# Operands in PSUM for one MLP and a modulation, other places for early products and for lower parts: a two-layer diffusion backbone

## The chip, the core and the metric

The kernel runs on one core of a Trainium2 chip. The core has five engines that work side by side, each through its own list of instructions in order: TensorE (PE in the profile, with its weight loads as PEld), VectorE (DVE), ScalarE (ACT), GpSimd (POOL) and SyncE (SP), which here only issues DMAs. They pass work on by semaphores, and they share two on-chip memories: SBUF, and PSUM, into whose banks of 128 x 512 floats the matmuls write. The metric is the device time of one execution in microseconds (us).

## The reference

A batch of one with 1024 latent tokens and 256 context tokens, width 1024, goes through two layers. Each layer derives six vectors for the latents and six for the context from a condition vector (`mod_l`, `mod_c`), normalises and modulates, mixes tokens (layer 0: a convolution module; layer 1: grouped attention), adds the gated result, and then runs an MLP with squared ReLU, again modulated and gated. After the last layer the context is dropped. Cut to what the change touches:

```python
sc = jax.nn.silu(c)
scc = jax.nn.silu(c_ctx)
for i in range(DEPTH):                                   # DEPTH = 2
    mod_l = jnp.split(sc @ w_mod[i] + b_mod[i], 6, axis=-1)
    mod_c = jnp.split(scc @ w_mod[i] + b_mod[i], 6, axis=-1)
    ...                                                  # norm, conv (0) or attention (1)
    ...
def sq_relu_mlp(h, w1, w2):                              # width 1024 -> 4096 -> 1024
    return jnp.square(jax.nn.relu(h @ w1)) @ w2
```

## The kernel before

**Three products for one.** Activations lie with channels on the 128 partitions and tokens along the free axis. Every large matmul is done in a float format that keeps only part of a float32, so each operand is held in two parts: the high part (a copy by ACT into that format) and the lower part (value minus high part). A product is then three matmuls: high x high, lower x high, high x lower (`mm3`, `prod`). For weights, `unit` (line 189) loads a 128 x 1024 tile `raw` by a DMA on SP, ACT writes the high part (line 205), and POOL the lower part (line 208) into `wsp` or, for each sixth unit, into `wx`. For activations the lower part is made on DVE or POOL.

**Layer 0** goes over three blocks b of up to 432 tokens. The convolution of a block (`conv_block`) is 31 taps on DVE (line 550), accumulated in PSUM banks named `cv`. The MLP (`mlp`, line 417 on) goes in eight chunks c of four hidden tiles f: for each f the product lands in a PSUM bank `ps`; ACT does the Relu into `r` and two Squares: one rounded into the high part `ht` (tile `hb` in the profile), one in full into `s`; DVE writes the lower part s - ht into `hb` (line 433). Then PE multiplies `hb` with `w2`, and DVE adds the gated sums to the stream `X` (line 455). PE takes its operands in program order, so a late `hb` or a late `X` (which frees a bank) holds PE up.

**The modulation of layer 1** is no matmul. `mods` (line 336) spreads the condition over all partitions (`sc`, 128 x 1024, Silu at line 341) and, for each 128 x 512 piece of the weights (`rawh`, loaded at line 347, three buffers), has DVE multiply it with half of `sc` and sum along the free axis (line 356, which the profile lists as a custom operation, with a short one that reads out the sum). 128 of them run as background work beside the MLP of block b = 1: a generator, `modq`, yields the estimated DVE time of each step and `pump` resumes it at fixed places of the foreground code. So the order on each engine is fixed when the program is built. Small additions and multiplications of 128 x 8 (lines 360, 331, 334) end each of the eight vectors.

**The MLP of layer 1** (`mlp1`, line 1186) forms its products by a scheme with seven half-size products instead of eight, on operands named B11, B21, T1, T3, T2, B22 and T4. While the second normalisation (`norm1`, line 1252 on, background work) prepares T1 to T4, PE runs "early" products for the first eight hidden tiles j: a first half with B11 into bank `b1`, copied to `p1` by ACT (line 1308), and a second half with B21 that goes on in the same bank. The second half of j-1 comes behind the first half of j. In the main loop `w1_ops` issues loads and splits with a priority that places them `AH1` = 190 places earlier than the code stands.

**The last product** (`ff2`, line 1407) goes over four chunks and, in each, over the seven operands. For each operand two activation tiles `tf` (list `tu`) and two weight tiles `raw` (list `wu`) are split: ACT writes the high part (line 1421) and DVE or POOL the lower part (line 1422, 128 x 1024). PE multiplies (line 1180), and DVE adds banks to sums (lines 1427, 1429). Which engine makes a lower part is set by two expressions at lines 1463 and 1475; G is POOL, V is DVE.

Of the kernel before, what the change touches and what calls it, by code (L numbers as in the profile page):

```python
# [117 lines left out]
NP = NF // 2  # L118
CP2 = 4
NPRO = 8  # L120
AH1, AH2 = 190, 200
PB = 2.5
OPS = ("B11", "B21", "T1", "T3", "T2", "B22", "T4")

# [1 line left out]
class Kern:  # L126
# [209 lines left out]
    def mods(self, i1, chunks, cond, dst):  # L336

        nc = self.nc
        sc = self.t("sc", [P, D], "sc")
        nc.sync.dma_start(out=sc, in_=self.A[cond].broadcast_to([P, D]))  # L340
        nc.scalar.activation(sc, sc, AF.Silu)
        units = [(j, u, z) for j in chunks for u in range(8) for z in range(2)]

        def load(i):
            j, u, z = units[i]
            raw = self.t(("ks", "vt", "sb")[i % 3], [P, 512], "rawh")
            nc.sync.dma_start(out=raw, in_=self.A["wmod1"][j * 8 + u, :, z * 512:z * 512 + 512])
            return raw
        raws = [load(0), load(1)]
        for i, (j, u, z) in enumerate(units):  # L350
            if i + 2 < len(units):
                raws.append(load(i + 2))
            if u == z == 0:
                part = self.t("mp", [P, 2, 8], "mp")
            raw = raws.pop(0)
            nc.vector.tensor_tensor_reduce(raw, raw, sc[:, z * 512:z * 512 + 512], 1.0, 0.0, ALU.mult, ALU.add,  # L356
                                           accum_out=part[:, z, u:u + 1])
            yield MQ
            if u == 7 and z:
                nc.vector.tensor_tensor(part[:, 0], part[:, 0], part[:, 1], ALU.add)  # L360
                self.mod_done(i1, j, dst, part[:, 0])
                self.mdone.add((i1, cond, j))
                yield 0.2
# [53 lines left out]
    def mlp(self, i, X, h, N, segs, gates, budget, hook=None, done=None, eng=None, off=False, each=None,  # L417
# [3 lines left out]
        for c in range(NF // CH):  # L421
            hT = []
            for f in range(c * CH, c * CH + CH):
                w = self.unit(self.A["w1"][i, f], eng)
                ps = self.psm()
                self.mm3(ps[:, :N], self.kpairs(w, h, N))
                r = self.t("tmp", [P, 512], "r")
                s = self.t("tmp", [P, 512], "s")
                ht = self.hts[f % 4]
                nc.scalar.activation(r[:, :N], ps[:, :N], AF.Relu)  # L430
                nc.scalar.activation(ht[:, 0, :N], r[:, :N], AF.Square)
                nc.scalar.activation(s[:, :N], r[:, :N], AF.Square)  # L432
                nc.vector.tensor_tensor(ht[:, 1, :N], s[:, :N], ht[:, 0, :N].bitcast(F32), ALU.subtract)  # L433
                hT.append(ht)
                self.pump(budget)
                if each:
                    each()
# [87 lines left out]
    def conv_block(self, b):  # L525
# [8 lines left out]
        for c2 in range(0, KT, 2):  # L534
# [17 lines left out]
            for z in range(2):  # L552
                v = u[:, c2 + z, off + 30:off + 30 + N]
                if c2 + z == 0:
                    nc.scalar.activation(vs[:, :N], v, AF.Copy)
                else:
                    nc.gpsimd.tensor_tensor(vs[:, :N], vs[:, :N], v, ALU.add)
        yield G3[2]
        mu = self.ps("rb", "mu")
        nc.tensor.matmul(mu[:, :N], lhsT=self.onesd, rhs=vs[:, :N], start=True, stop=True)  # L560
# [55 lines left out]
    def layer0(self):  # L616
# [3 lines left out]
        self.h1, self.u, self.udone, self.s1, self.X, self.h2 = {}, {}, {}, {}, {}, {}  # L620

        self.mdone = set()
        self.cc = self.t("cc", [P, KT, 2], "cc")
        nc.sync.dma_start(out=self.cc, in_=self.A["ccol"])
        nc.scalar.activation(self.cc, self.cc, AF.Silu)
# [560 lines left out]
    def mlp1(self, at, pre, r0):  # L1186
# [108 lines left out]
            nc.sync.dma_start(out=self.hd[OPS.index(o), :, j], in_=s)  # L1295

        halves = lambda w: [(lambda k: w[0](k), lambda k: w[1](k)), (lambda k: w[0](4 + k), lambda k: w[1](4 + k))]
        late = None

        def second(j, b1, a12):  # L1300
            self.prod(b1, a12, piece("B21"), False)
            hidden(b1, self.t("tmp", [P, 512], "s11"), j, "B11")
        for j in range(NPRO):
            a11, a12 = halves(self.unit(self.A["w1"][1, 2 * j]))
            b1 = self.ps("mm", "b1")
            p1 = self.t("tmp", [P, 512], "p1")
            self.prod(b1, a11, piece("B11"), True)
            nc.scalar.activation(p1, b1, AF.Copy)
            nc.sync.dma_start(out=self.p1d[:, j], in_=p1)
            if j:  # L1310
                self.pump(PB)
                second(*late)
            late = j, b1, a12
            if j:
                self.pump(PB)
        second(*late)
        while self.bg:
            self.pump(8.0)

# [1 line left out]
        ring = [work[:, 4 + i] for i in range(4)]  # L1321

        def w1_ops(j):
            with self.tc.high_priority(AH1):
                ra, rb = [self.t("raw", [P, 1024], "raw") for _ in range(2)]
                nc.sync.dma_start(out=ra, in_=self.A["w1"][1, 2 * j])
                nc.sync.dma_start(out=rb, in_=self.A["w1"][1, 2 * j + 1])
# [79 lines left out]
    def ff2(self, X):  # L1407
# [40 lines left out]
        for c in range(NC):  # L1448
# [6 lines left out]
            for what, y, first in ending if last else order:  # L1455
                with self.tc.high_priority(AH2):
                    tu, wu = [], []
                    z = {"B11": 0, "B21": 1, "T4": 3}.get(what)
                    for i in range(2):
                        f = self.t("raw", [P, 1024], "tf")  # L1460
                        nc.sync.dma_start(out=f.rearrange("p (i n) -> p i n", i=2),
                                          in_=self.hd[OPS.index(what), :, c * CP2 + 2 * i:c * CP2 + 2 * i + 2])
                        tu.append(unit(f, V if c == 0 and what == "B11" and i else G))
                    for i in range(2):
                        h = slice(1024 * i, 1024 * i + 1024)
                        s = S[:, h]
# [5 lines left out]
                            V.tensor_tensor(s, raw[1][:, h], s, ALU.subtract)  # L1472
                        elif what == "T3":
                            V.tensor_tensor(s, raw[0][:, h], raw[2][:, h], ALU.subtract)  # L1474
                        wu.append(unit(s if z is None else raw[z][:, h], G if z in (1, 3) or i and (z == 0 or last and what == "T1") else V))
                    xs = []
                    if c == NC - 2 and what in blocks:
                        _, blk, r = blocks[what]
# [143 lines left out]
```

## Time and profile before

| what | us |
|---|---|
| time, median of 3 runs (lowest, highest) | 2970.96 (2965.88, 2971.44) |
| the profiled execution: its time | 2970.38 |
| its span, first to last instruction | 2968.6 |
| PE busy in the span | 2779.6 |
| DVE busy | 2156.9 |
| POOL busy | 1709.4 |
| ACT busy | 1486.3 |

The profile is of one execution. The page gives each engine's busy time, the span in 40 slices, the chain of work that ended last, and the costliest groups of instructions, each with the idle time of its engine just before it and what released it. Beside the page the trace answers narrower questions: the waits of one engine by what ended them, the busy times of a window, the durations of one line's instructions, and the timeline. An idle engine costs nothing unless PE, the busiest one, waits for it later. A few rows in which matmuls, the main work, are seen to fill most of each slice but the first (each digit is the busy share of a fortieth of the span, in tenths; PEclk is the granted clock of TensorE, also in tenths):

```profile
PE   7999999999888899998998899999999889999999
PEclk9999999999998999999999999999999999999999
```

The first four slices in a row where PE's digit is 8 are 742 to 1039 us: the stretch in which the modulation of layer 1 runs beside the MLP of block 1.

### The profile page before, as it was taken

The numbers are of one execution on the slowest core, as the hardware profiler recorded it, in microseconds if no ns is written. First come the engines' busy times: TensorE is split into PE (matmuls) and PEld (weight loads), VectorE is DVE, ScalarE is ACT, GpSimd is POOL, SyncE is SP. The second block draws the span as 40 slices with busy tenths as digits, with TensorE's granted clock in tenths as the row PEclk, the third lists the DMA queues.
The fourth block names the chain that finished last, engine by engine and source line by source line (L and its number), as shares of the span: only waits on it lengthen the run. The fifth ranks groups of instructions, "written<-read, shape, count | busy, mean of one in ns | idle before, by whom it ended". The sixth has DMA issues, their size and how long they took to land. (4 is left out here: it accounts for less than half of the span.)

```text
span 2968.6 us, 36063 instructions
## 1 busy us (share of the span) xinstructions
PE 2779.6 (94%) x12634; PEld 2338.2 (79%) x12634; DVE 2156.9 (73%) x3224; ACT 1486.3 (50%) x2383; POOL 1709.4 (58%) x959
## 2 busy tenths in 40 slices
PE   7999999999888899998998899999999889999999
PEld 3778999999888899887886677776677667878877
DVE  3888999997678644447457889986987645458696
ACT  4543554545344353435435577664675544454332
POOL 3777666676456564434434466654666555567664
PEclk9999999999998999999999999999999999999999
DMA  7454333243765624343444411122106555475452
GB/s 242 165 177 156 126 119 116 93 145 115 246 213 200 208 100 165 112 138 118 151 143 145 135 26 22 22 79 78 22 8 207 158 177 169 138 247 176 152 178 93
DMA packets 176582, 406.67 MB, mean 137 GB/s; under 512 B 21328, under 2 KB 64848, under 8 KB 174352
## 3 DMA queue, kind: packets, MB, share of 16 engines
q1 hardware_dynamic: 176400, 404.37, 41.9%
q8 instruction: 99, 1.62, 0.2%
q14 instruction: 83, 0.68, 0.1%
HBM read 343.49 MB, written 60.82 MB: 136 GB/s over the span
## 5 line engine op out<-in xcount | busy, mean ns | idle before, releaser
L208 POOL TENSOR_TENSOR wsp<-raw,wsp 128x1024 fp32r<-128x1024 f32 x254 | 628.2, 2483 | 447.0 <-ACT wsp L205 418.0
L216 PE MATMUL ps<-h,wsp 128*128 128x432 f32 (+1 forms) x2832 | 578.6, 362 | 12.3 <-DVE X L455 4.6
L216 PEld LDWEIGHTS ps<-h,wsp 128*128 128x128 f32 x2832 | 536.8, 191 | 52.5 <-issue 15.0
L205 ACT ACTIVATE wsp<-raw 128x1024 fp32r<-128x1024 f32 x291 | 306.2, 1056 | 308.7 <-PE ps L216 182.7
L216 PE MATMUL ps<-hb,wsp 128*128 128x432 f32 (+1 forms) x1920 | 404.6, 365 | 25.4 <-DVE hb L433 21.4
L550 DVE SCALAR_TENSOR_TENSOR cv<-u,vec,cv 128x464 f32<-128x464 f32 (+2 forms) x696 | 422.8, 670 | 6.1 <-ACT cv L547 4.6
L216 PEld LDWEIGHTS ps<-hb,wsp 128*128 128x128 f32 x1920 | 368.4, 193 | 46.9 <-DVE hb L433 25.9
L1075 POOL TENSOR_TENSOR p<-e,p 128x512 fp32r<-128x512 f32 x223 | 307.3, 1391 | 165.6 <-ACT p L1073 102.6
L1180 PE MATMUL b<-u 128*128 128x512 f32 x1344 | 309.2, 392 | 7.1 <-DVE sums L1429 5.0
L1180 PEld LDWEIGHTS b<-u 128*128 128x128 f32 x1344 | 254.2, 189 | 62.0 <-DVE sums L1429 3.0
L1068 ACT ACTIVATE e<-sT 128x512 f32<-128x512 f32 x320 | 185.9, 596 | 123.7 <-PE sT L1066 102.6
L433 DVE TENSOR_TENSOR hb<-s,hb 128x432 fp32r<-128x432 f32 (+1 forms) x96 | 129.7, 1352 | 102.4 <-ACT s L432 102.2
L1422 POOL TENSOR_TENSOR u<-tf,u 128x1024 fp32r<-128x1024 f32 x55 | 154.4, 2828 | 82.3 <-ACT u L1421 55.6
L1030 DVE TENSOR_REDUCE m<-s 128x1 f32<-128x512 f32 (+1 forms) x336 | 192.1, 591 | 11.1 <-PE s L1028 10.1
L356 DVE CUSTOM_DVE_ANT_0 rawh<-rawh,sc 128x512 f32<-128x512 f32 x128 | 144.6, 1152 | 61.9 <-DMA rawh<-in_wmod 51.8
L455 DVE SCALAR_TENSOR_TENSOR X<-ps,m,X 128x432 f32<-128x432 f32 (+2 forms) x144 | 81.1, 586 | 109.6 <-PE ps L216 109.4
L1071 DVE CAST p<-e 128x512 fp32r<-128x512 f32 x160 | 115.9, 725 | 32.1 <-ACT e L1068 27.9
L216 PE MATMUL ps<-h,wx 128*128 128x432 f32 (+1 forms) x624 | 131.4, 368 | 6.3 <-DVE X L455 6.3
L208 POOL TENSOR_TENSOR wx<-raw,wx 128x1024 fp32r<-128x1024 f32 x45 | 111.4, 2475 | 38.9 <-ACT wx L205 38.2
L1180 PE MATMUL b<-T,wsp 128*128 128x512 f32 x576 | 133.3, 389 | 0.0
L216 PEld LDWEIGHTS ps<-h,wx 128*128 128x128 f32 x624 | 121.5, 196 | 14.1 <-issue 7.3
L1082 PE MATMUL O<-p,half 128*128 128x512 f32 x320 | 127.8, 400 | 0.0
(315 smaller groups left out, 5415.6 us busy)
## 6 DMA issues: line engine op xcount, KB each, us to landing
raw<-in_w SPq DMA_DIRECT2D x232, 512.0 KB, 3.4
raw<-in_pw SPq DMA_DIRECT2D x72, 512.0 KB, 3.4
rawh<-in_wmod SPq DMA_DIRECT2D x128, 256.0 KB, 3.3
tf<-hd SPq DMA_DIRECT2D x56, 512.0 KB, 3.6
raw<-in_qkv SPq DMA_DIRECT2D x36, 512.0 KB, 3.4
rawp<-in_wmod SPq DMA_DIRECT2D x32, 512.0 KB, 4.4
raw<-in_w2s SPq DMA_DIRECT2D x16, 1024.0 KB, 7.0
hd<-t SPq DMA_DIRECT2D x48, 256.0 KB, 2.3
```

The lines of the kernel that those rows point to most:

```text
L205: nc.scalar.activation(hi(c, n), raw[:, c * P:(c + n) * P], AF.Copy)
L208: (eng or nc.gpsimd).tensor_tensor(lo(c, n), raw[:, c * P:(c + n) * P], hi(c, n).bitcast(F32), ALU.subtract)
L216: self.nc.tensor.matmul(ps, lhsT=(wh, wl, wh)[t], rhs=(ah, ah, al)[t], start=first and i == t == 0, stop=last and i == n - 1 and t == 2)
L356: nc.vector.tensor_tensor_reduce(raw, raw, sc[:, z * 512:z * 512 + 512], 1.0, 0.0, ALU.mult, ALU.add, accum_out=part[:, z, u:u + 1])
L433: nc.vector.tensor_tensor(ht[:, 1, :N], s[:, :N], ht[:, 0, :N].bitcast(F32), ALU.subtract)
L550: nc.vector.scalar_tensor_tensor(dst, src, tap, acc[z][:, :N], ALU.mult, ALU.add)
L1030: nc.vector.reduce_max(m3[:, qt, j, c:c + 1], s[:, :w], axis=AX.X)
L1068: nc.scalar.activation(e, s, AF.Exp, scale=0.125)
L1075: (nc.vector if u % lm == lm - 1 else nc.gpsimd).tensor_tensor(p[:, 1], e, p[:, 0].bitcast(F32), ALU.subtract)
L1082: nc.tensor.matmul(O[1], lhsT=self.half, rhs=p[:, 0], start=a, stop=False)
L1180: self.nc.tensor.matmul(ps, lhsT=w[t % 2](k), rhs=(ah, ah, al)[t], start=first and k == t == 0, stop=k == 3 and t == 2, skip_group_check=True)
L1422: eng.tensor_tensor(w[:, 1], src, w[:, 0].bitcast(F32), ALU.subtract)
```

## The change

It has four parts.

1. In `mlp` the tile `s` is gone. The second Square is written back into the PSUM bank `ps` from which the Relu was read, and the subtraction reads it there. 96 subtractions change their first operand from SBUF to PSUM.
2. In `mods` the Silu of the condition is written to two PSUM banks named `cv` (`scp`) as two activations of 512 columns, and the 128 reductions read it there. Before that the generator waits (`while not self.taps`) until the taps of the last convolution block have been issued, since they use these banks.
3. In `mlp1` the second halves wait in a list and follow two products later than their first halves instead of one; `AH1` is 115 for the first eight units and 190 for the others.
4. In `ff2` the lower part of the second activation tile (i = 1) is made by DVE for every operand, where before it was only so for B11 of the first chunk; of the weight tiles only B11's second goes to POOL, where before all of B21 and T4, the second of B11 and, in the last chunk, the second of T1 did. POOL's share of the lower parts falls from 76 to 32, DVE's grows from 36 to 80.

```diff
-AH1, AH2 = 190, 200
+AH1, AH2 = (115, 190), 200
...
-        nc.scalar.activation(sc, sc, AF.Silu)
+        while not self.taps:
+            yield None
+
+        scp = [self.ps("cv", "scp") for _ in range(2)]
+        for z in range(2):
+            nc.scalar.activation(scp[z], sc[:, z * 512:z * 512 + 512], AF.Silu)
...
-            nc.vector.tensor_tensor_reduce(raw, raw, sc[:, z * 512:z * 512 + 512], 1.0, 0.0, ALU.mult, ALU.add,
+            nc.vector.tensor_tensor_reduce(raw, raw, scp[z], 1.0, 0.0, ALU.mult, ALU.add,
...
-                s = self.t("tmp", [P, 512], "s")
...
-                nc.scalar.activation(s[:, :N], r[:, :N], AF.Square)
-                nc.vector.tensor_tensor(ht[:, 1, :N], s[:, :N], ht[:, 0, :N].bitcast(F32), ALU.subtract)
+                nc.scalar.activation(ps[:, :N], r[:, :N], AF.Square)
+                nc.vector.tensor_tensor(ht[:, 1, :N], ps[:, :N], ht[:, 0, :N].bitcast(F32), ALU.subtract)
...
+        self.taps = b == 2
...
-        late = None
+        late = []
...
+            late.append((j, b1, a12))
             if j:
                 self.pump(PB)
-                second(*late)
-            late = j, b1, a12
+            if len(late) > 2:
+                second(*late.pop(0))
             if j:
                 self.pump(PB)
-        second(*late)
+        for x in late:
+            second(*x)
...
-            with self.tc.high_priority(AH1):
+            with self.tc.high_priority(AH1[j >= NPRO]):
...
-                        tu.append(unit(f, V if c == 0 and what == "B11" and i else G))
+                        tu.append(unit(f, V if i else G))
...
-                        wu.append(unit(s if z is None else raw[z][:, h], G if z in (1, 3) or i and (z == 0 or last and what == "T1") else V))
+                        wu.append(unit(s if z is None else raw[z][:, h], G if i and what == "B11" else V))
```

The lines of the changed file lie 1 to 8 further down: 356 becomes 361, 433 becomes 437, 455 becomes 459, 1180 becomes 1186, 1208 becomes 1214, 1422 becomes 1430 and 1429 becomes 1437.

DVE in the modulation stretch, at a place where one chunk of a vector ends (about 780 us in the profile of before). `m_75` is the vector that is being finished, `mp` the partial sums, `X` the stream of the MLP:

```order
L360 TENSOR_TENSOR mp<-mp 128x8
L356 ISA rawh,mp<-rawh,sc 128x512
L356 ISA mp 128x1
L331 TENSOR_TENSOR m_75<-mp,vec 128x8
L334 SCALAR_TENSOR_TENSOR m_75<-m_75,vec 128x8
L356 ISA rawh,mp<-rawh,sc 128x512
L356 ISA mp 128x1
L455 SCALAR_TENSOR_TENSOR X<-ps,m_73,X 128x176
L455 SCALAR_TENSOR_TENSOR X<-ps,c_74,X 128x256
```

and the same place after the change:

```order
L365 TENSOR_TENSOR mp<-mp 128x8
L361 ISA rawh,mp<-rawh,scp 128x512
L361 ISA mp 128x1
L331 TENSOR_TENSOR m_75<-mp,vec 128x8
L334 SCALAR_TENSOR_TENSOR m_75<-m_75,vec 128x8
L361 ISA rawh,mp<-rawh,scp 128x512
L361 ISA mp 128x1
L459 SCALAR_TENSOR_TENSOR X<-ps,m_73,X 128x176
L459 SCALAR_TENSOR_TENSOR X<-ps,c_74,X 128x256
```

Nothing moved here: only the operand `sc` (SBUF) became `scp` (PSUM), and the line numbers of `mods` and `mlp` shifted.

PE among the early products, about 2335 us in the profile of before. `B11_...` and `B21_...` are the operands of first and second halves; `b1_19997` is the bank of j = 4, `b1_19941` of j = 3, `b1_20055` of j = 5:

```order
L1180 MATMUL b1_19997<-B11_19510,wsp_19994 128x512 x6
L1180 MATMUL b1_19997<-B11_19511,wsp_19994 128x512 x6
L1180 MATMUL b1_19941<-B21_19512,wsp_19938 128x512 x6
L1180 MATMUL b1_19941<-B21_19513,wsp_19938 128x512 x6
L1180 MATMUL b1_20055<-B11_19510,wsp_20052 128x512 x6
L1180 MATMUL b1_20055<-B11_19511,wsp_20052 128x512 x6
L1180 MATMUL b1_19997<-B21_19512,wsp_19994 128x512 x6
L1180 MATMUL b1_19997<-B21_19513,wsp_19994 128x512 x6
```

and after the change, where `b1_19894` is the bank of j = 4, `b1_19952` of j = 5, `b1_19768` of j = 2 and `b1_19838` of j = 3:

```order
L1186 MATMUL b1_19894<-B11_19423,wsp_19891 128x512 x6
L1186 MATMUL b1_19894<-B11_19424,wsp_19891 128x512 x6
L1186 MATMUL b1_19768<-B21_19425,wsp_19765 128x512 x2
L1186 MATMUL b1_19768<-B21_19426,wsp_19765 128x512 x6
L1186 MATMUL b1_19952<-B11_19423,wsp_19949 128x512 x6
L1186 MATMUL b1_19952<-B11_19424,wsp_19949 128x512 x6
L1186 MATMUL b1_19838<-B21_19425,wsp_19835 128x512 x6
L1186 MATMUL b1_19838<-B21_19426,wsp_19835 128x512 x6
L1186 MATMUL b1_19894<-B21_19425,wsp_19891 128x512 x6
L1186 MATMUL b1_19894<-B21_19426,wsp_19891 128x512 x6
```

The second half of j = 4 stands behind the first of j = 5 in both, with the second half of j = 3 now between them.

POOL at the same time; `X_...`, `t_...`, `T_...` and `u_...` are the normalised stream and the pieces of the second normalisation, `wsp` a weight. Before:

```order
L1208 TENSOR_TENSOR u_19917<-X_19448,u_19917 128x512
L1208 TENSOR_TENSOR T_19911<-t_19919,T_19911 128x512
L1208 TENSOR_TENSOR T_19913<-X_19448,T_19913 128x512
L208 TENSOR_TENSOR wsp<-raw,wsp 128x1024
L1208 TENSOR_TENSOR T_19911<-t_19959,T_19911 128x512
```

and after:

```order
L1214 TENSOR_TENSOR u_19814<-X_19361,u_19814 128x512
L1214 TENSOR_TENSOR T_19808<-t_19816,T_19808 128x512
L1214 TENSOR_TENSOR T_19810<-X_19361,T_19810 128x512
L1214 TENSOR_TENSOR u_19814<-X_19361,u_19814 128x512
L1214 TENSOR_TENSOR T_19808<-t_19856,T_19808 128x512
L208 TENSOR_TENSOR wsp<-raw,wsp 128x1024
```

The weight's lower part now stands behind two more pieces of the normalisation instead of ahead of them.

DVE in the third chunk of the last product; `sums_...` are the accumulated sums, `b` a PSUM bank, `u` a lower part, `tf` an activation tile, `raw_...` a weight tile. Before:

```order
L1429 TENSOR_TENSOR sums_22213<-b,sums_22213 128x512 x3
L1429 TENSOR_TENSOR sums_22215<-b,sums_22215 128x512 x2
L1422 TENSOR_TENSOR u<-raw_23232,u 128x1024
L1429 TENSOR_TENSOR sums_22215<-b,sums_22215 128x512 x2
L1429 TENSOR_TENSOR sums_22214<-b,sums_22214 128x512 x6
L1422 TENSOR_TENSOR u<-sums_22215,u 128x1024
```

and after:

```order
L1437 TENSOR_TENSOR sums_22126<-b,sums_22126 128x512
L1430 TENSOR_TENSOR u<-tf,u 128x1024
L1437 TENSOR_TENSOR sums_22128<-b,sums_22128 128x512 x2
L1430 TENSOR_TENSOR u<-raw_23145,u 128x1024
L1437 TENSOR_TENSOR sums_22128<-b,sums_22128 128x512 x2
L1430 TENSOR_TENSOR u<-tf,u 128x1024
L1437 TENSOR_TENSOR sums_22127<-b,sums_22127 128x512 x2
L1430 TENSOR_TENSOR u<-raw_23146,u 128x1024
```

Lower parts that were POOL's now stand between the additions that read out the banks.

More of the change, by code (lines that the diff above doesn't have):

```diff
@@ L622, in layer0 @@
         self.mdone = set()
+        self.taps = False
         self.cc = self.t("cc", [P, KT, 2], "cc")
```

## The prediction

> **What bounds the kernel now.** I began with the page's busy shares and then read the waits of PE over the whole span.
>
> ```profile
> PE 2779.6 (94%) x12634; PEld 2338.2 (79%) x12634; DVE 2156.9 (73%) x3224; ACT 1486.3 (50%) x2383; POOL 1709.4 (58%) x959
> PE ps L216 <- DVE hb L433: 22.3, 12, 4.6
> PE ps L216 <- DVE X L455: 15.6, 7, 4.6
> PE b L1180 <- ACT p L1308: 8.1, 2, 7.1
> PE b L1180 <- DVE sums L1429: 5.0, 2, 2.6
> PE b L1180 <- DVE sums L1427: 1.5, 1, 1.5
> ```
> The matmuls fill 94% of the span and the change removes none of them. It can therefore only win PE's waits (here: us in total, times, longest), and what slow clock follows them, or lose by making new ones. The waits that its four parts touch are these five rows. So I cut the span into the stretches where they fall: the modulation of layer 1 (743 to 1034), the early products (2302 to 2357) and the last product (2640 on).
>
> ```profile
> 743.00:1034.00 291.00, 253.90 (x1206) 235.27 (x1205) 222.10 (x386) 116.37 (x187) 170.56 (x80) 0.94 0.65 219
> 2302.00:2357.00 55.00, 45.91 (x183) 36.73 (x184) 37.62 (x46) 33.16 (x55) 27.15 (x16) 0.88 0.53 162
> 2640.00:2968.60 328.60, 317.64 (x1382) 260.85 (x1380) 244.77 (x213) 115.28 (x116) 207.95 (x78) 0.99 0.49 164
> ```
> The columns are the stretch's length, the busy time (instructions) of PE, PEld, DVE, ACT and POOL, the granted clock, the DMA share and GB/s. In the first stretch PE idles 37 us and the clock is 0.94. The waits there, of PE and of DVE:
>
> ```profile
> PE ps L216 <- DVE hb L433: 17.5, 7, 4.6
> PE st L251 <- DVE acc L284: 4.1, 1, 4.1
> DVE rawh L356 <- DMA rawh<-in_wmod: 51.8, 41, 4.5
> DVE X L455 <- PE ps L216: 4.1, 6, 1.0
> ```
> All of the 15.6 us at `X` quoted above lie in this stretch too, so PE waits for DVE 17.5 + 15.6 = 33.1 us at `hb` and `X`; DVE waits for PE only 4.1. DVE is the slow partner here: in this stretch it does 128 reductions of line 356 beside the MLP's work, in one fixed order. Why it is slow stands in two groups that differ by where the operands lie:
>
> ```profile
> L356 DVE CUSTOM_DVE_ANT_0 rawh<-rawh,sc x128: 677/692/2915, 751.2 to 1033.5; 128x512 f32<-128x512 f32 x128
> L356 DVE CUSTOM_DVE_ANT_0 rawh<-rawh,sc 128x512 f32<-128x512 f32 x128 | 144.6, 1152 | 61.9 <-DMA rawh<-in_wmod 51.8
> L433 DVE TENSOR_TENSOR hb<-s,hb 128x432 fp32r<-128x432 f32 x24 | 29.1, 1216 | 8.3 <-ACT s L432 8.3
> L455 DVE SCALAR_TENSOR_TENSOR X<-ps,m,X x144: 384/651/669, 413.8 to 1545.6; 128x432 f32<-128x432 f32 x64, 128x416 f32<-128x416 f32 x40, 128x176 f32<-128x176 f32 x40
> L1429 DVE TENSOR_TENSOR sums<-b,sums x72: 674/682/695, 2698.4 to 2926.7; 128x512 f32<-128x512 f32 x72
> ```
> (The triple is shortest/median/longest in ns; the third row is the stretch's part of L433.) With both tensors in SBUF, the reduction takes 692 ns in the median and up to 2915, mean 1152. With one in PSUM, L455 and L1429 never pass 669 and 695. L1429 runs in the last product, where POOL is as busy (208 of 328.6 us) as in the modulation stretch (171 of 291). The timeline of one bad spot shows what the long ones go with:
>
> ```profile
> 930.74 14.04 POOL L208 TENSOR_TENSOR wsp<-raw,wsp 128x1024 fp32r<-128x1024 f32 x5
> 930.74 0.68 DVE L356 CUSTOM_DVE_ANT_0 rawh<-rawh,sc 128x512 f32<-128x512 f32 x1
> 934.16 2.90 DVE L356 CUSTOM_DVE_ANT_0 rawh<-rawh,sc 128x512 f32<-128x512 f32 x1
> 937.00 2.80 DVE L433 TENSOR_TENSOR hb<-s,hb 128x432 fp32r<-128x432 f32 x1
> 942.50 2.74 DVE L433 TENSOR_TENSOR hb<-s,hb 128x432 fp32r<-128x432 f32 x1
> 945.30 1.45 PE L216 MATMUL ps<-hb,wsp 128*128 128x432 f32 x3 [4.59 <-DVE hb L433]
> ```
> Five POOL subtractions in a row take 14.04 us, 2.81 each, and beside them each DVE operation takes as long as one of them. PE then waits 4.59 us for `hb`.
>
> **Parts 1 and 2: Squares and condition in PSUM.** Count and place of DVE's instructions stay; 96 subtractions and 128 reductions get one PSUM operand. I price a reduction at 0.692 (its own median, beside L1429's 0.682 at the same width) and a subtraction at 0.651 (L455's median, same width). DVE gains 128 x (1.152 - 0.692) = 59 us and 24 x (1.216 - 0.651) = 14, 73 of its 222 in the stretch. The bounds are nothing (the operand does not matter: a rival) and 75 (shortest times).
>
> [...]
>
> What of the 73 reaches PE? Not all of its waits stand behind long DVE operations.
>
> ```profile
> 758.58 0.66 PE L216 MATMUL ps<-hb,wsp 128*128 128x432 f32 x2 [1.85 <-DVE hb L433]
> 976.11 1.42 PE L216 MATMUL ps<-h,wx 128*128 128x432 f32 x3 [3.49 <-DVE X L455]
> 767.58 0.83 PE L216 MATMUL ps<-hb,wsp 128*128 128x432 f32 x3 [1.48 <-DVE X L455]
> 998.77 1.09 PE L216 MATMUL ps<-hb,wsp 128*128 128x432 f32 x2 [4.47 <-DVE hb L433]
> 995.36 1.38 DVE L356 CUSTOM_DVE_ANT_0 rawh<-rawh,sc 128x512 f32<-128x512 f32 x1 [1.37 <-DMA rawh<-in_wmod]
> 998.11 0.60 DVE L433 TENSOR_TENSOR hb<-s,hb 128x432 fp32r<-128x432 f32 x1
> ```
> Following each of the eleven waits over 1 us back along DVE, I find six behind contended operations, 19.2 us in all (the first row and the second are the first and the last of them), and five, 12.0 us in all, behind reductions that waited for their weights (third and fourth rows). At 998.11 the subtraction took only 0.60; it stood behind reductions whose DMA was late. Of the six I take 16 of 19.2, because a few two-SBUF operations stay in their chains, as this one, with 8 columns:
>
> ```profile
> 781.04 2.25 DVE L360 TENSOR_TENSOR mp<-mp 128x8 f32<-128x8 f32 x1
> SPq L347 <- DVE mp L356: 115.3, 93, 6.6
> SPq L195 <- POOL wsp L208: 71.3, 30, 9.9
> ```
> Of the five I take half, 6: SP's queue issues a reduction's load only when an older reduction has freed its buffer (115.3 us of waiting), so faster reductions issue earlier; but loads queued on the same SP behind POOL (71.3) stay late. Together 22 of 33.1. The slow clock comes on top: 0.94 over 291 us is 17 us of lost clock, partly lost while PE waited anyway; I take 8, in the proportion of the waits that go. So 30 in this stretch (bounds 0 and 33 + 17 = 50). Before it the same line cost 22.3 - 17.5 = 4.8 us; I take 1.
>
> The reductions now wait until the convolution's taps have freed two PSUM banks. The first reduction ran at 751.2 and had waited for ACT anyway; the work order puts the modulation behind the taps, so I count that wait at 0, with 5 us as its bound if the convolution ends late. The bank of an MLP unit is held until the subtraction instead of the Relu; the bank's next user needs that `hb` anyway: 0.
>
> **Part 3: early products.**
>
> ```profile
> 2326.61 2.82 POOL L208 TENSOR_TENSOR wsp<-raw,wsp 128x1024 fp32r<-128x1024 f32 x1
> 2327.12 2.86 DVE L1274 TENSOR_TENSOR t<-X,h 128x512 f32<-128x512 f32 x1
> 2334.86 0.58 ACT L1308 ACTIVATE p<-b 128x512 f32<-128x512 f32 x1
> 2335.49 16.65 PE L1180 MATMUL b<-B,wsp 128*128 128x512 f32 x60 [7.06 <-ACT p L1308]
> ```
> PE stands 7.06 us until ACT has copied `p` of the fifth early product; ACT works in order, behind the second normalisation. The new order puts more products between a first and its second half, but the second half that waits here, of j = 4, stays the eleventh product in PE's order, so depth alone gives nothing. The POOL queue gives something: the weight's lower part (2.82) falls behind the normalisation's, and the copy may come one such step earlier. I take 3 (bounds -4, the weight late for the product that needs it, and +11: both 8.1 waits and the clock, 0.88 here). The shorter lead of 115 places for eight units moves loads and splits later; PE has work between; 0 (-2 to +3).
>
> **Part 4: the last product.** 44 lower parts go from POOL to DVE.
>
> ```profile
> L1422 DVE TENSOR_TENSOR u<-sums,u x31: 1207/1226/3437, 2669.1 to 2933.7; 128x1024 fp32r<-128x1024 f32 x31
> L1422 POOL TENSOR_TENSOR u<-tf,u x55: 2389/2862/3412, 2634.6 to 2935.7; 128x1024 fp32r<-128x1024 f32 x55
> L1422 POOL TENSOR_TENSOR u<-raw,u x20: 2382/2415/3392, 2638.4 to 2942.8; 128x1024 fp32r<-128x1024 f32 x20
> ```
> DVE takes 44 x 1.226 = 54 us more at the median, and 245 + 54 = 299 fits in 328.6. Beside fewer POOL operations its own long ones get rarer. PE waits only 5.0 + 1.5 us for this line of work; I take 0 (bounds -12, as DVE's order now has parts ahead of the additions that free banks, and +8, the waits and a little clock).
>
> **Sum.** 30 + 1 + 3 + 0 = 34 us. The profiled execution took 2970.4 (span 2968.6), the median of the runs 2971.0, so both give 2936.
>
> **The rivals.**
> - **The weights' loads become the bound** of the modulation stretch. For: 51.8 us of DVE's waits are already for `rawh`, and a faster DVE meets the same SP queue. Against: 115.3 us of that queue is waiting for DVE itself. Then about half of the six contended waits are won and none of the five: 10, with 2 to 3 of clock and 3 elsewhere: 2955. Chance 0.18.
> - **Nearly all waits of the stretch go,** with most of the clock: 33 + 14, 4 from line 433 before it and 4 from the early products, 55: 2915. For: 73 us of DVE time are twice the waits. Chance 0.14.
> - **DVE becomes the bound of the last product: slower.** The parts that move read two SBUF tensors and still run beside 32 POOL operations; the longest on DVE took 3.437. If all 44 did, DVE would need 44 x 3.437 = 151 us against the 328.6 - 244.8 = 84 that it has free: 67 lost, 34 won, 3003. It decides from 84 + 34 = 118 us, 2.7 each. Against: the median of 31 such parts is 1.226 beside more POOL work. Chance 0.05. [...]
> - **The change does not do what it says:** the new PSUM operands leave DVE as slow, because what blocks is the write side. L455 and L1429 also write SBUF and stay short, which speaks against. Then 3 us are left: 2967. Chance 0.05.
>
> **How the numbers follow.** The forecast has 0.58. Range 2908 to 2962: it holds the forecast's case, the load rival, and half of the high one; 0.17 is outside. A measurement of this kernel tells about 0.2%, 6 us, from no change: faster 0.90, same 0.05, slower 0.05.
>
> **What would show it.** L361 near 0.69 and L437 near 0.65 with no long ones; `hb` and `X` waits of 743 to 1034 near 11 us and clock near 0.97; the wait at `p` near 4; waits at `sums` in the last product no larger than 6.5. I am wrong if DVE's waits for `rawh` grow by as much as it saves, if lines 361 or 437 stay bimodal, or if `sums` waits pass 15 us.

## The result, and the profile after

The changed kernel takes 2922.86 us (median of 4 runs, 2921.92 to 2927.67), the kernel before 2971.2 beside it: ratio 0.9842, 95% interval 0.9824 to 0.9860, by the ratio about 47 us faster. The forecast was 2936, and the time lies inside its range. Its stages, however, came out quite otherwise than the sum had them.

The page of the changed kernel (busy shares), and those of PE's waits over its whole span that bear on the change (us, times, longest); `st` is a small matmul that sums squares for a norm, and the last row is from the kernel before, for `st`:

```profile
PE 2759.9 (95%) x12634; PEld 2320.2 (79%) x12634; DVE 2046.4 (70%) x3268; ACT 1481.9 (51%) x2386; POOL 1568.6 (54%) x915
```

```profile
PE b L1186 <- ACT work L1376: 20.0, 7, 6.2
PE st L251 <- DVE acc L284: 14.3, 7, 5.8
PE ps L216 <- DVE X L459: 11.3, 7, 3.3
PE ps L216 <- DVE hb L437: 8.6, 8, 2.4
PE b L1186 <- ACT p L1314: 4.0, 1, 4.0
PE b L1186 <- ACT s L1299: 3.1, 1, 3.1
```

```profile
PE st L251 <- DVE acc L284: 19.9, 9, 4.1
```

`hb` fell from 22.3 to 8.6, `X` from 15.6 to 11.3, and the waits for `sums` are gone. `st` fell too, from 19.9 to 14.3, which no step of the prediction had; of `p` 4.0 are left, with a new wait of 3.1 for `s`.

PE runs 12634 matmuls in both kernels, so the start of the n-th of them can be compared. How far the changed kernel is ahead at such a matmul is its start before minus its start after. Between the five points of the table, and to the end, this grew as follows:

| from, to (us, before) | forecast | measured |
|---|---|---|
| 0 to 743, up to the modulation | 1 | 11.4 |
| 743 to 1034, modulation stretch | 30 | 20.2 |
| 1034 to 1310, MLP of block 2 begins | 0 | 10.8 |
| 1310 to 2303, attention | 0 | -0.5 |
| 2303 to 2640, early products, hidden loop | 3 | -4.3 |
| 2640 to the end, last product | 0 | 10.9 |
| sum | 34 | 48.5 |

Kernels that do not touch a stage differ there by up to some 5 us (part 2 alone, whose first reduction runs at 746.5, is 5.2 ahead at 743), so single entries below that say little. The windows of the changed kernel for the modulation stretch, the stage behind it and the last product (columns as in the prediction):

```profile
733.00:1007.00 274.00, 250.75 (x1221) 233.68 (x1221) 149.32 (x391) 116.04 (x192) 153.88 (x81) 0.97 0.70 233
1007.00:1270.00 263.00, 263.00 (x1329) 247.80 (x1328) 88.90 (x146) 123.35 (x193) 129.02 (x63) 1.00 0.40 131
2602.00:2920.10 318.10, 314.24 (x1383) 259.07 (x1382) 267.29 (x257) 115.79 (x117) 88.65 (x34) 1.00 0.50 170
```

DVE's busy time in the modulation stretch fell from 222 to 149, 73 us as forecast, because the long operations of the two lines vanished altogether. All executions of the two lines (shortest/median/longest in ns):

```profile
L361 DVE CUSTOM_DVE_ANT_0 rawh<-rawh,scp x128: 655/686/692, 738.6 to 987.4; 128x512 f32<-128x512 f32 x128
L437 DVE TENSOR_TENSOR hb<-ps,hb x96: 574/602/609, 399.3 to 1483.2; 128x432 fp32r<-128x432 f32 x64, 128x416 fp32r<-128x416 f32 x32
```

Longest 692 in place of 2915, 609 in place of 2799. What is left in the stretch, in the waits of PE and DVE and at one place of the timeline:

```profile
PE ps L216 <- DVE X L459: 11.0, 6, 3.3
PE ps L216 <- DVE hb L437: 6.5, 5, 2.4
DVE rawh L361 <- DMA rawh<-in_wmod: 95.6, 70, 8.8
```

```profile
921.71 0.69 DVE L361 CUSTOM_DVE_ANT_0 rawh<-rawh,scp 128x512 f32<-128x512 f32 x1 [5.45 <-DMA rawh<-in_wmod]
922.32 0.60 DVE L437 TENSOR_TENSOR hb<-ps,hb 128x432 fp32r<-128x432 f32 x1
922.98 1.39 PE L216 MATMUL ps<-hb,wsp 128*128 128x432 f32 x4 [2.01 <-DVE hb L437]
```

DVE's waits for weights grew from 51.8 to 95.6 us: more than half of the 73 came back as waiting. Here the subtraction that PE needs stands one place behind a reduction for whose load DVE had waited 5.45 us.

### The profile page after: what moved, and what is told of

It reads as the page before. It is cut to its first block, busy times and chain, and to the rows that moved or that the text cites. A ratio compares the mean times of both kernels' runs of the same rounds, so it can differ in the third digit from the quotient of the medians.

```text
span 2920.1 us, 35997 instructions
## 1 busy us (share of the span) xinstructions
PE 2759.9 (95%) x12634; PEld 2320.2 (79%) x12634; DVE 2046.4 (70%) x3268; ACT 1481.9 (51%) x2386; POOL 1568.6 (54%) x915
## 5 line engine op out<-in xcount | busy, mean ns | idle before, releaser
L208 POOL TENSOR_TENSOR wsp<-raw,wsp 128x1024 fp32r<-128x1024 f32 x254 | 616.8, 2438 | 447.0 <-ACT wsp L205 405.5
L216 PE MATMUL ps<-hb,wsp 128*128 128x432 f32 (+1 forms) x1920 | 400.4, 363 | 20.1 <-DVE X L459 11.3
L1430 POOL TENSOR_TENSOR u<-tf,u 128x1024 fp32r<-128x1024 f32 x28 | 76.7, 2738 | 174.3 <-ACT u L1429 174.3
L361 DVE CUSTOM_DVE_ANT_0 rawh<-rawh,scp 128x512 f32<-128x512 f32 x128 | 86.5, 684 | 103.0 <-DMA rawh<-in_wmod 95.6
L1077 DVE CAST p<-e 128x512 fp32r<-128x512 f32 x160 | 116.0, 726 | 31.0 <-ACT e L1074 26.9
L437 DVE TENSOR_TENSOR hb<-ps,hb 128x432 fp32r<-128x432 f32 (+1 forms) x96 | 57.4, 598 | 111.6 <-ACT ps L436 111.4
L1186 PEld LDWEIGHTS b<-T,wsp 128*128 128x128 f32 x576 | 108.1, 188 | 23.4 <-POOL wsp L1341 0.8
L216 PE MATMUL ps<-h,wx 128*128 128x432 f32 (+1 forms) x624 | 125.4, 356 | 0.0
```

The source lines that it names most:

```text
L208: (eng or nc.gpsimd).tensor_tensor(lo(c, n), raw[:, c * P:(c + n) * P], hi(c, n).bitcast(F32), ALU.subtract)
L216: self.nc.tensor.matmul(ps, lhsT=(wh, wl, wh)[t], rhs=(ah, ah, al)[t], start=first and i == t == 0, stop=last and i == n - 1 and t == 2)
L361: nc.vector.tensor_tensor_reduce(raw, raw, scp[z], 1.0, 0.0, ALU.mult, ALU.add, accum_out=part[:, z, u:u + 1])
L1077: nc.vector.tensor_copy(p[:, 0], e)
L1186: self.nc.tensor.matmul(ps, lhsT=w[t % 2](k), rhs=(ah, ah, al)[t], start=first and k == t == 0, stop=k == 3 and t == 2, skip_group_check=True)
```

## The experiments

### Each part alone

The diff of each is its piece of the change, shown above.

**Part 1, the second Square in PSUM.**

> Only part 1, the second Square in PSUM. Theory (an operand in PSUM takes the subtraction out of the contention with POOL): line 433's successor has no duration above 0.61 us anywhere, the gains of the changed kernel before 743 us (11) and from 1034 to 1310 (11) appear here in full, because the condition is not touched there; in the modulation stretch the 128 reductions stay long in part and take over some of the contention, so 3 to 8 us there. Sum 25 to 30: 2941 to 2946. Rival (the gain comes from both operands only together, DVE having the same number of long operations as before): under 10, above 2961.

Measured: 2952.9, ratio 0.9926 (0.9913 to 0.9938), 22 us. By stages: 13.1 up to 743, 3.1 in the modulation stretch, 10.8 from 1034 to 1310. The subtraction is at 0.61 at most. In its stretch the reductions stay long, and of PE's 33.1 us at `hb` and `X` 26.9 are left, now mostly at `X`:

```profile
PE ps L216 <- DVE X L454: 18.7, 9, 4.8
PE ps L216 <- DVE hb L432: 8.2, 4, 3.5
```

```profile
L356 DVE CUSTOM_DVE_ANT_0 rawh<-rawh,sc x128: 672/693/2894, 737.7 to 1017.3; 128x512 f32<-128x512 f32 x128
L356 DVE CUSTOM_DVE_ANT_0 rawh<-rawh,sc 128x512 f32<-128x512 f32 x128 | 141.0, 1123 | 73.2 <-DMA rawh<-in_wmod 61.5 <-ACT sc L341 11.1
```

A little under what was expected, and mostly in stages where the prediction had put 1 us or nothing.

**Part 2, the condition in PSUM.**

> Only part 2, the condition in PSUM. Theory: reductions at 0.69 us throughout, line 433 stays long in the stretch; waits at hb stay near 17 us there and those at X fall; nothing changes outside the stretch. 10 to 16 us: 2955 to 2961. Rival (weights' loads bound the stretch already): under 5 us, above 2966.

Measured: 2958.0, ratio 0.9947 (0.9935 to 0.9959), 16 us; 11.3 of its profile's gain lies in the modulation stretch. Outside it, where nothing was expected, the profile shows 5.2 gained up to 743 and 4.4 lost in the attention. The reductions now take 691 ns at most, and the subtractions stay long. Their group in the stretch, and the longest of them with POOL beside it:

```profile
L438 DVE TENSOR_TENSOR hb<-s,hb 128x432 fp32r<-128x432 f32 x24 | 40.2, 1675 | 12.0 <-ACT s L437 12.0
919.71 10.80 DVE L438 TENSOR_TENSOR hb<-s,hb 128x432 fp32r<-128x432 f32 x1
920.48 12.29 POOL L208 TENSOR_TENSOR wsp<-raw,wsp 128x1024 fp32r<-128x1024 f32 x5
```

Freeing one of the two kinds of operation leaves the other in POOL's way: a reduction takes 1123 ns in the mean with part 1 alone (1152 before), a subtraction 1675 with part 2 alone (1216 before; 1675 is 1278 without the one of 10.80 us). In the stretch parts 1 and 2 alone give 3.1 and 11.3 us, both with the others 16 to 20. That they give more together than added up is within the noise.

**Part 3, early products and lead** (`AH1`), and its later second halves alone (the lead stays at 190 places):

> Only part 3, later second halves and the shorter lead. By the two traces, counted at the same matmul, the changed kernel loses 4 us between 2302 and 2405: 2973 to 2976, and the loss lies there. Rival (that loss comes from the other parts, by loads that now collide with the early products; part 3 alone gains as predicted): 2968.

> The kernel before with only the later second halves of part 3, the lead left at 190 places. Theory (the new order takes most of the wait at p and gives it back at a new wait, for ACT's read of the previous bank): the wait at p near 4 in place of 7.1, a new wait of about 3 ahead of it, no gain at the matmul that stood at 2357. Rival (the loss lies in the lead alone): 3 us gained there.

Measured: part 3 2975.6, ratio 1.0006 (0.9997 to 1.0016). Later second halves alone, in one profiled run: 2974.0 beside 2973.9. PE in the kernel with part 3 alone:

```profile
2326.74 5.74 PE L1180 MATMUL b<-B,wsp 128*128 128x512 f32 x24 [3.10 <-ACT s L1293]
2337.82 2.50 PE L1180 MATMUL b<-B,wsp 128*128 128x512 f32 x5 [5.34 <-ACT p L1308]
```

The wait of 7.06 became two, 3.10 and 5.34: with the new order PE also needs a bank that ACT has not yet read (`s`), and ACT, in its order, is late at both behind the same second normalisation (shortly before it copies `p` it waits 3.31 us for DVE's `t` of that work). The later halves alone show the same pair (3.08 and 5.86). No gain shows, and the loss of 4 us that was expected is not shown either: the interval reaches from 1 us gained to 5 lost. The lead by itself was not run.

**Part 4, the lower parts of the last product.**

> Only part 4, 44 lower parts from POOL to DVE. By the two traces the changed kernel gains 11 us in the last product: three waits at sums go (6.5) and the slow clock behind them (3 to 4). Alone: 2960 to 2962. Rival (the three waits went because the work before arrives otherwise, by parts 1 to 3): within 3 us of the kernel before.

Measured: 2968.0, ratio 0.9973 (0.9961 to 0.9984), 8 us; in its profile 10.9 are gained in the last product and 3 lost in the modulation stretch, which it does not touch. DVE and PE of the kernel before at one of the three waits:

```profile
2869.19 3.44 DVE L1422 TENSOR_TENSOR u<-sums,u 128x1024 fp32r<-128x1024 f32 x1
2872.66 3.29 DVE L1470 TENSOR_TENSOR sums<-sums,raw 128x1024 f32<-128x1024 f32 x1
2875.88 0.68 DVE L1429 TENSOR_TENSOR sums<-b,sums 128x512 f32<-128x512 f32 x1
2876.70 1.54 PE L1180 MATMUL b<-u 128*128 128x512 f32 x4 [2.37 <-DVE sums L1429]
```

and the same operations in the changed kernel:

```profile
2826.68 1.22 DVE L1430 TENSOR_TENSOR u<-sums,u 128x1024 fp32r<-128x1024 f32 x1
2827.93 1.23 DVE L1478 TENSOR_TENSOR sums<-sums,raw 128x1024 f32<-128x1024 f32 x1
2829.07 0.68 DVE L1437 TENSOR_TENSOR sums<-b,sums 128x512 f32<-128x512 f32 x1
```

Two long operations in a row had made the addition late; both are short here, with fewer POOL operations to meet (32 for 76). Some long ones are left elsewhere (up to 3.44 us), but PE no longer waits for `sums`, in the run with part 4 alone either.

**All without part 3.**

> The changed kernel without part 3. Part 3 alone gave a ratio of 1.0006 (0.9997 to 1.0016). Theory: it has no value here either, 2920 to 2926 beside the changed kernel's 2922.9. Rival: together with the others it costs the 4 us that the two traces show between 2302 and 2640, then 2916 to 2919.

Measured: 2924.6, ratio 0.9839 (0.9820 to 0.9858), against 0.9842 with it. The theory holds: part 3 has no value that shows.

### All lower parts of the last product on DVE

This too is without part 3, so the kernel to compare with is the one above.

```diff
-                        tu.append(unit(f, V if i else G))
+                        tu.append(unit(f, V))
...
-                        wu.append(unit(s if z is None else raw[z][:, h], G if i and what == "B11" else V))
+                        wu.append(unit(s if z is None else raw[z][:, h], V))
```

> The changed kernel without part 3, and all 112 lower parts of the last product on DVE, none on POOL. With no POOL work beside it each part costs 1.21: DVE's busy time in the last product is 267 - 122 + 112 x 1.21 = 280 us less some 15 for other operations that are no longer slowed, of a stretch of 318. Theory: it still fits, DVE is no bound; time within 4 us of the kernel with 32 on POOL. Rival (DVE as bound, the slower case of the prediction): PE waits for sums or u appear, 15 us or more lost.

Measured: 2922.0, ratio 0.9823 (0.9803 to 0.9843). Its last product:

```profile
2600.00:2918.00 318.00, 314.32 (x1386) 259.77 (x1384) 257.80 (x287) 116.10 (x117) 5.81 (x3) 1.00 0.50 170
```

With all 112 parts DVE is busy for 258 of 318 us, less than the 267 with 80 parts beside POOL's 32: the parts rise from 119 to 131 us only, as one takes 1.23 us in the mean in place of 1.53, and the rest of DVE's work falls from 149 to 127. PE waits for nothing there, and the slower rival is refuted even with 76 parts moved in place of 44.

### Why part 1 gained outside the modulation

Line 433 costs little outside the stretch (4.8 us of PE's waits), yet part 1 gained 24 there, waits and the slow clock behind them (from 1034 to 1310 the granted clock rose from 0.98 to 1.00; in the kernel before it was 0.50 from 1230 to 1234, right behind a wait of 3.73 us for `st`). A second effect offered itself: without `s` the ring of five temporaries (`tmp`), from which the squares `sq` of the next norm are taken too, has a user less. The first test leaves both operands in SBUF and takes `s` out of the ring:

```diff
-                s = self.t("tmp", [P, 512], "s")
+                s = self.t("sown", [P, 512], "s")
...
-BUFS = {"w8": 5, "raw": 3, "rawm": 1, "xu": 3, "hl": 2, "hb": 1, "tmp": 5, "acc": 3, "sc": 1, "qs": 1, "ks": 1,
+BUFS = {"w8": 5, "raw": 3, "rawm": 1, "xu": 3, "hl": 2, "hb": 1, "sown": 1, "tmp": 4, "acc": 3, "sc": 1, "qs": 1, "ks": 1,
```

> The kernel before, with the tile s in a buffer of its own in SBUF and the ring of temporaries cut from five to four, so that the other users keep a ring without s, as with part 1, while both operands of the subtraction stay in SBUF. Theory (contention by operand): line 433 keeps a longest duration near 2.8 us and a mean near 1.35, and at the end of the first two MLP blocks (matmuls to 743 and to 1310 of the kernel before) nothing like the 10 and 11 us of part 1 alone is gained. Rival (part 1 helps because s leaves the ring): most of these 21 us appear.

Measured (one profiled run): 2976.4, as the kernel before. Line 433 stays long, up to 2798, and up to 743 nothing is gained. It loses 8.2 us in the modulation stretch and 7.6 in the attention; `s` now has one buffer only, for which ACT waits 32.8 us in all. But from 1034 to 1310 it gains 10.2 us, nearly as much as part 1. I had expected nothing like it. PE's waits in this stage, in the kernel before and with `s` on its own:

```profile
PE st L251 <- DVE acc L284: 5.8, 2, 3.7
PE ps L216 <- DVE hb L433: 0.4, 1, 0.4
```

```profile
PE ps L216 <- DVE hb L433: 0.3, 1, 0.3
```

ACT and DVE of the kernel before, at its wait of 3.73 for `st` near 1226:

```profile
1219.64 0.53 ACT L430 ACTIVATE r<-ps 128x432 f32<-128x432 f32 x1 [2.10 <-PE ps L216]
1220.37 1.06 ACT L205 ACTIVATE wsp<-raw 128x1024 fp32r<-128x1024 f32 x1 [0.20 <-DMA raw<-in_w]
...
1222.24 1.75 ACT L281 ACTIVATE sq<-x 128x384 f32<-128x384 f32 x4
1224.42 1.00 ACT L281 ACTIVATE sq<-x 128x384 f32<-128x384 f32 x2 [0.42 <-DVE hb L433]
```

```profile
1222.37 2.01 DVE L433 TENSOR_TENSOR hb<-s,hb 128x432 fp32r<-128x432 f32 x1 [3.57 <-ACT s L432]
1224.31 5.04 DVE L282 TENSOR_TENSOR acc<-acc,sq 128x384 f32<-128x384 f32 x6
```

and of the kernel with `s` on its own, at the same place:

```profile
1226.77 0.53 ACT L430 ACTIVATE r<-ps 128x432 f32<-128x432 f32 x1 [2.03 <-PE ps L216]
1227.20 0.52 ACT L281 ACTIVATE sq<-x 128x384 f32<-128x384 f32 x1
```

```profile
1227.74 0.56 DVE L282 TENSOR_TENSOR acc<-acc,sq 128x384 f32<-128x384 f32 x1 [1.75 <-ACT sq L281]
1228.65 0.61 DVE L433 TENSOR_TENSOR hb<-s,hb 128x432 fp32r<-128x432 f32 x1 [0.35 <-ACT s L432]
1229.18 2.43 DVE L282 TENSOR_TENSOR acc<-acc,sq 128x384 f32<-128x384 f32 x5
```

Before, the first `sq` stands behind both Squares of the MLP, the fifth waits until DVE gives `s` back, and DVE's six additions take 5.04 us, the later ones beside a POOL subtraction that starts at 1226.44. With `s` out of the ring, the first `sq` moves up to just behind the Relu, the additions take 2.99 us, and PE does not wait. The counter-test is part 1 with a tile `s` that still goes round the ring:

```diff
                 nc.scalar.activation(ps[:, :N], r[:, :N], AF.Square)
-                nc.vector.tensor_tensor(ht[:, 1, :N], ps[:, :N], ht[:, 0, :N].bitcast(F32), ALU.subtract)
+                nc.scalar.activation(s[:, 0:1], r[:, 0:1], AF.Copy, scale=0.0)
+                nc.vector.scalar_tensor_tensor(ht[:, 1, :N], ps[:, :N], s[:, 0:1], ht[:, 0, :N].bitcast(F32), ALU.add, ALU.subtract)
```

> As e1_square (second Square in PSUM), but a tile s of the ring of temporaries is still taken for each hidden tile: ACT writes one column of zeros into it, and DVE adds that column in the subtraction, so that s is given back when it was before. Theory after e9_own (part 1 has two effects: the operand leaves the contention, worth its share up to 743 and in the modulation stretch; and the ring without s lets the scheduler place the squares of the next norm earlier on ACT, worth the 11 us from 1034 to 1310): the subtraction stays at 0.6 us, the gain of e1_square up to 743 stays, and that from 1034 to 1310 goes, so about 2961 and waits at st of 3 us or more between 1050 and 1250. Rival (contention alone explains part 1): as e1_square, 2952, no such wait.

Measured: 2966.1, ratio 0.9972 (0.9960 to 0.9985), 8 us. From 1034 to 1310 it gains 3.2, with these waits there; its subtraction is never long:

```profile
PE st L251 <- DVE acc L284: 4.4, 2, 2.7
```

```profile
L434 DVE SCALAR_TENSOR_TENSOR hb<-ps,s,hb x96: 634/658/669, 399.4 to 1520.7; 128x432 fp32r<-128x432 f32 x64, 128x416 fp32r<-128x416 f32 x32
```

So most of part 1's 10.8 there is the ring (10.2 with the ring alone, 3.2 with the operand alone). Up to 743 it gains 5.1 where part 1 gained 13.1 and the same was expected here, and 5.1 is no more than part 2 alone shows there. With the ring alone nothing was gained. PE's waits from 384 us to the end of that stage point to both: at `st` they are 2.5 us before, 0.3 with part 1 and with the ring alone, 2.1 in the counter-test; at `hb` 4.4 before, 2.0 with part 1, 9.5 with the ring alone and 2.9 in the counter-test. How these 13.1 divide stays open. The counter-test also adds an ACT operation of 0.19 us per tile, and `s` on its own leaves a ring of four: the split is not exact.

### What holds the rest of the modulation stretch

Two more buffers, the halves of `sc`, which is free once its Silu stands in PSUM; without part 3:

```diff
-            raw = self.t(("ks", "vt", "sb")[i % 3], [P, 512], "rawh")
+            raw = self.t(("ks", "vt", "sb")[i % 5], [P, 512], "rawh") if i % 5 < 3 else sc[:, (i % 5 - 3) * 512:(i % 5 - 2) * 512]
...
-        raws = [load(0), load(1)]
+        raws = [load(i) for i in range(4)]
...
-            if i + 2 < len(units):
-                raws.append(load(i + 2))
+            if i + 4 < len(units):
+                raws.append(load(i + 4))
```

> The changed kernel without part 3, with five buffers for the weights of the modulation in place of three (the two halves of sc, free once its Silu has been written to PSUM, are the other two), and loads issued four reductions ahead. Theory (what is left of PE's waits in the modulation stretch, 11.0 at X, 6.5 at hb and 5.8 at st, stands behind reductions whose load is late): DVE's waits for rawh fall from 96 us to under 40, PE's in the stretch from 23 to under 8, and the time falls by 12 to 20 against the kernel with three buffers: about 2905. Rival (the loads stand in SP's queue behind loads that wait for POOL, so issuing ahead does not help): DVE's waits stay above 80, time within 4 us of three buffers.

Measured: 2916.1, ratio 0.9802 (0.9784 to 0.9820), 8.5 under three buffers. The stretch gains 25.5 against 16.0. DVE's waits there, and SP's:

```profile
DVE rawh L361 <- DMA rawh<-in_wmod: 35.6, 25, 5.9
DVE sc L361 <- DMA sc<-in_wmod: 21.1, 14, 6.1
```

```profile
SPq L195 <- POOL wsp L208: 104.4, 33, 12.9
SPq L352 <- DVE mp L361: 65.8, 74, 7.0
```

The direction is right, the size is not: 57 us of DVE's waits, not under 40, and 20 of PE's in the stretch, not under 8. SP now waits mostly for POOL's lower parts, with the modulation's loads queued behind. So these loads went to another queue, to ACT's as shown here, or in the same way to POOL's (`nc.gpsimd`):

```diff
-            nc.sync.dma_start(out=raw, in_=self.A["wmod1"][j * 8 + u, :, z * 512:z * 512 + 512])
+            nc.scalar.dma_start(out=raw, in_=self.A["wmod1"][j * 8 + u, :, z * 512:z * 512 + 512])
```

> As e8_five, with the modulation's loads issued from ACT in place of SP. In e8_five DVE still waited 57 us for these loads and PE 20 us in the stretch, while SP waited 104 us for POOL's lower parts of other weights. Theory (the loads stand behind others in SP's queue): DVE's waits for them fall under 20, PE's under 10, time 4 to 8 under e8_five's 2916. Rival (an issue on ACT waits for a free buffer and holds up ACT's high parts behind it, or the DMA engines are full): no gain or a loss against e8_five.

> As e11_actq, with the loads issued from POOL. Theory: POOL's own lower parts are 2.4 us long and in order, so its loads wait behind them about as on SP: within 3 us of e8_five. Rival: off SP is what matters, as good as e11_actq.

Measured: from ACT 2909.5, ratio 0.9775 (0.9757 to 0.9792); from POOL 2948.5, ratio 0.9905 (0.9888 to 0.9921). From ACT the stretch gains 36.1 and PE waits 4.0 and 3.5 us at `X` and `hb`, where it had waited 6.8 and 5.7. One wait of 3.6 for ACT's high part of `hb` is new, so 11.8 us are left in all, not under 10. The time fell as expected, but not as the theory had it: DVE's waits for loads stayed at 56 in place of under 20. That these loads now seldom stand ahead of what PE needs would fit, but was not followed; nor was what the other weights' loads, without these on SP, gained by it. From POOL both expectations fail. POOL spends 0.54 us on each issue and waits 43 us ahead of them, mostly for buffers, and SP's waits for POOL's lower parts (`wsp`) are 197.3 us, against 160.1 with the loads from ACT:

```profile
L352 POOL DMA_DIRECT2D rawh<-in_wmod x76 | 41.1, 542 | 15.2 <-DVE mp L361 11.1 <-DVE c L331 0.9 <-DVE mp L365 0.9
L352 POOL DMA_DIRECT2D sc<-in_wmod x49 | 26.6, 543 | 28.2 <-DVE mp L361 14.8 <-ACT scp L346 10.5 <-DVE m L331 1.9
```

The kernel with loads from ACT, five buffers and no part 3 is the fastest of those run: 2.25% under the kernel before, where the change takes 1.58%.

## Why the prediction was right, and where it was not

- **Bound and mechanism of parts 1 and 2: right.** DVE was the slow partner of the modulation stretch, and the PSUM operand ends its contention with POOL: its operations are no longer held up while POOL works (154 of the stretch's 274 us in the changed kernel): the longest took 692 and 609 ns, 2915 and 2799 before. Priced at 692 and 651 ns, measured 686 and 602 (medians); 73 us of DVE time forecast, 73 measured. Part 1, part 2 and the counter-test each show it for their own operation. The operand in PSUM did not lengthen the reduction itself: 686 ns with it, 692 without (medians). Of the 224 operations that now read one operand from PSUM and one from SBUF none passed 692 ns.
- **What reaches PE in the stretch: mis-sized, 20 for 30.** Of the waits at `hb` and `X`, 17.5 us were left where I had 11, and `st` rose from 4.1 to 5.8: 14 us of waits went where I had 22, and 6 of PE's busy time, as the clock rose from 0.94 to 0.97, where I had 8. The load rival was half true: I had taken half of the five load-bound waits as won, and instead DVE's waiting for loads grew by 44 us. More buffers and another queue won 20 us more in that stretch than the same kernel without them.
- **"Count and place of DVE's instructions stay", with 1 us before the stretch and nothing behind it: wrong by 21 us.** I had followed the operand and not the tile. Dropping `s` frees a place in a ring that another chain uses, and the order on ACT outside the stretch changed. For the 10.8 us from 1034 to 1310 the runs show this; for the 11.4 up to 743 the ring and the operand are not told apart. The first could have been read before: the wait `sq ... <-DVE hb L433` stands in the trace.
- **Early products: 3 forecast, no gain measured,** inside the bounds. That depth alone does not help was right, as far as one run tells. The wait at `p` fell to 3.99 in the changed kernel, near the 4 that I expected, but a new wait of 3.08 for ACT's `s` stands ahead of it, together 7.07 for the 7.06 before. The sum had no term for such a wait. That POOL's new order brings the copy earlier is not shown.
- **Last product: 0 forecast with 8 as its most, 10.9 measured.** DVE's lower parts did take 53 us more (70 for 36 of them, 122 for 80), close to the price (54), but that is luck: one takes 1.53 us in the mean, where I had taken 1.226, and the 36 before took 1.94. The waits of 5.0 and 1.5 at `sums` went completely, and so did the slow clock behind them (0.99 to 1.00), which I had allowed "a little".
- The forecast had 10 us too much in the stretch and 7 in the early products, and 21 and 11 too little elsewhere; these partly cancelled, and that the total is nearer than its terms is luck.

## What to carry to other kernels

When DVE and POOL run side by side, look at the longest duration of a line, not only its mean (here 2915 ns beside a mean of 1152), and move one operand of what stands ahead of PE's needs into PSUM (here the longest fell to 692); but free all operations of that stretch, since here the kind that was left stayed long (up to 2894 ns with part 1 alone, up to 10.80 us with part 2 alone). When a temporary disappears, ask which chain shares its ring, and compare the order on every engine, not only where the operand changed. When an engine becomes faster, price what feeds it: here 44 of 73 us returned as waits for loads. More buffers took 40 of them away again, and another queue then cut PE's waits, though not DVE's.

## What had not been expected of the hardware

A DMA issue from POOL occupied it for 0.54 us in the mean, where an issue of the same loads from SP took 0.33 us in the kernel before and in the changed one (medians). Issued from POOL, beside its own work, these loads cost 39 us against issuing them from ACT (2948.5 and 2909.5 us).

A subtraction with both operands in SBUF was once held for 10.80 us, while POOL ran five of its own, of 128x1024, without a gap in 12.29 us (part 2 alone); in the kernel before and in the changed one no DVE instruction took more than 3.44 us.

Giving DVE more work in the last product (112 lower parts for 80) lowered its busy time from 267 to 258 us: with almost no POOL work beside it (5.8 us, against 88.7), one of its lower parts took 1.23 us in the mean in place of 1.53, and the rest of its work 127 us in place of 149.
